# Turning each key head once, and copying it twice into the rows that the scores read

## The chip, the cores and the metric

The kernel runs on one core of one Trainium2 chip. The metric is the time of one execution on the device in microseconds (us). Five engines work side by side and meet at semaphores: PE multiplies matrices, DVE and ACT work on vectors, POOL does a few small steps, and SP's queue issues most DMA transfers. PE writes only to PSUM, which has eight banks; ACT and DVE move the results from there to SBUF. SBUF and PSUM have 128 partitions, called rows here where a matmul contracts over them.

## The reference

The program is a two-layer transformer trunk of width 1024, applied to two sequences, one of 256 and one of 512 positions. Layer A is a windowed attention with 16 query heads and 4 key heads of size 64; layer B is a differential attention with 8 heads, each with two queries and two keys of size 64. A gated feed-forward network follows each. What the change touches is how the scores are formed:

```
q = apply_rope(q, cos, sin) * (HEAD_DIM ** -0.5)
k = apply_rope(k, cos, sin)
...
sc = einsum('bqkgd,bskd->bkgqs', qi, kb)          # layer A, four queries share a key head
sc = einsum('bqhcd,bkhcd->bhcqk', qi, k)          # layer B, c = 0, 1: two queries, two keys
p  = softmax(sc);  a = p[:, :, 0] - lam * p[:, :, 1]
```

## The kernel before, in words

The 768 positions stand in six tiles of 128: tiles 0 and 1 are the first sequence, tiles 2 to 5 the second. Every product is made from two parts of each operand, a rounded part ("hi") and the rest ("lo"): hi x hi, lo x hi and hi x lo (`product_steps`, lines 313 to 317).

`mixer_a` and `mixer_b` both run over units i = (head group, tile), 24 units in A and 48 in B. A unit multiplies the tile's activations by the head's weights (24 matmuls of 384 columns into one bank, called `pqa` in A and `pqb` in B). Its `end` then does four things: ACT copies the values out of the bank (line 589, line 787), DVE rotates queries and keys (`rope`, lines 530 to 536, into `qk`), ACT writes the hi parts into a tile `sp` and DVE the lo parts (lines 594 to 599 in A, 794 to 799 in B). Two units later `turn` lets PE transpose the columns of `sp`, 128 by 128 at a time, into two banks, `tk` for keys and `tq` for queries (trace names `tka`, `tqa`, `tkb`, `tqb`), and ACT and DVE copy them to SBUF, where the scores read them.

How the parts lie matters. A score product contracts over 128 rows. In A a transposed query holds its hi part in rows 0 to 63 and its lo part in rows 64 to 127; so the key must stand in both halves: `kh` holds the key's hi part twice, and one product with it gives (hi + lo) x hi; `kl` holds the key's lo part twice. In B a head's two queries stand as (hi, lo) and (lo, hi), and the tile `kk` (trace name `kb`) holds three blocks: key 0's hi part twice, key 1's hi part twice, and key 0's and key 1's lo parts one above the other. In B `score` makes two products over 128 rows, one for each key (line 828), and two over 64 rows, one in the upper and one in the lower half (line 831). Before the change the doubling is done in `sp`: the parts are written there twice, and each doubled block is transposed.

A program written in this way passes through a scheduler when it is built: it puts each engine's instructions in an order that follows the source and the scheduler's own idea of when operands are ready. So a change of one helper can move instructions of other steps too. An engine then works through its own list strictly in that order, and an instruction that waits holds up what stands behind it.

In B the source places a unit's attention steps by the table `plan` (line 887). The four scores of the second sequence need the keys of all of tiles 2 to 5, so the first of these scores stands shortly after the turn of tile 5, in the unit of the next head's tile 1: this is called the head's boundary here.

Of the kernel before, what the change touches and what calls it, by code (L numbers as in the profile page):

```python
# [17 lines left out]
P = 128  # L18
D = 1024
KT = D // P  # L20
HD = 64
# [25 lines left out]
def trunk(  # L47
# [519 lines left out]
    def mixer_a(gp, g_next, first_steps, o):  # L567
        with ExitStack() as st:
# [4 lines left out]
            def unit(i):  # L573

                gi, t = divmod(i, NT)
                first, n = seq_of(t)
                if t == 0:
                    wk[gi] = column_blocks(take(4), HALF)
                elif t in (2, 4):
                    free(6 - t // 2)  # L580
                pm = bank(f"pqa_{i}")
                steps = product_steps(pm[:, :HALF], [(htile(t, k), wk[gi][k]) for k in range(KT)])
                if t == NT - 1:
                    steps = releasing(steps, 4, 2)

                def end():
                    if t == first:
                        vv[gi, first] = ap.tile([P, n, HD], F32, tag=f"v{first}", name=f"va{gi}_{first}", bufs=2)
                    nc.scalar.copy(out=vv[gi, first][:, t - first], in_=pm[:, 320:384])
                    qk = ap.tile([P, 5, HD], F32, tag="qk", name=f"qk{i}", bufs=2)  # L590
                    rope(ap, qk, pm[:, :320].rearrange("p (n d) -> p n d", d=HD), 5, t, f"a{i}")

                    sp = ap.tile([P, 6, 2, HD], F32R, tag="sp", name=f"sp{i}", bufs=2)
                    nc.scalar.copy(out=sp[:, 0:4, 0], in_=qk[:, 0:4])
                    nc.scalar.copy(out=sp[:, 4], in_=qk[:, 4:5].broadcast_to([P, 2, HD]))
                    nc.vector.tensor_tensor(
                        out=sp[:, 0:4, 1], in0=qk[:, 0:4], in1=sp.bitcast(F32)[:, 0:4, 0], op=ALU.subtract)
                    nc.vector.tensor_tensor(
                        out=sp[:, 5], in0=qk[:, 4:5].broadcast_to([P, 2, HD]), in1=sp.bitcast(F32)[:, 4], op=ALU.subtract)

                    def turn():
                        if t == first:
                            kh[gi, first] = ap.tile([P, n * P], F32R, tag=f"kh{first}", name=f"kha{gi}_{first}")
                            kl[gi, first] = ap.tile([P, n * P], F32R, tag=f"kl{first}", name=f"kla{gi}_{first}")
                        q[i] = ap.tile([P, 4, P], F32R, tag="q", name=f"qa{i}", bufs=4)
                        tq, tk = ps.tile([P, 512], F32R, tag="ps", name=f"tqa{i}"), ps.tile([P, 512], F32R, tag="ps", name=f"tka{i}")
                        at = slice((t - first) * P, (t - first + 1) * P)
                        for j in range(2):
                            nc.tensor.transpose(tk[:, j * P:(j + 1) * P], sp[:, 4 + j].rearrange("p a d -> p (a d)"), ident_r)
                        for j in range(4):  # L610
                            nc.tensor.transpose(tq[:, j * P:(j + 1) * P], sp[:, j].rearrange("p a d -> p (a d)"), ident_r)
                        nc.scalar.copy(out=kh[gi, first][:, at], in_=tk.bitcast(F32)[:, 0:P])
                        nc.scalar.copy(out=kl[gi, first][:, at], in_=tk.bitcast(F32)[:, P:2 * P])
                        nc.scalar.copy(out=q[i].rearrange("p h n -> p (h n)"), in_=tq.bitcast(F32))

                    pending[i] = turn

                return steps + [end]
# [146 lines left out]
    def mixer_b(gp, g_next, first_steps, o):  # L765
        with ExitStack() as st:
# [5 lines left out]
            def unit(i):  # L772

                h, t = divmod(i, NT)
                first, n = seq_of(t)
                if t == 0:
                    wk[h] = column_blocks(take(4), HALF)
                    free(4)
                pm = bank(f"pqb_{i}")
                steps = product_steps(pm[:, :HALF], [(htile(t, k), wk[h][k]) for k in range(KT)])  # L780
                if t == NT - 1:
                    steps = releasing(steps, 4)

                def end():
                    if t == first:
                        vv[h, first] = ap.tile([P, n, P], F32, tag=f"v{first}", name=f"vb{h}_{first}", bufs=2)
                    nc.scalar.copy(out=vv[h, first][:, t - first], in_=pm[:, 256:384])
                    qk = ap.tile([P, 4, HD], F32, tag="qk", name=f"bqk{i}", bufs=2)
                    rope(ap, qk, pm[:, :256].rearrange("p (n d) -> p n d", d=HD), 4, t, f"b{i}")

                    sp = ap.tile([P, 5, 2, HD], F32R, tag="sp", name=f"bsp{i}", bufs=2)
                    s4 = sp.rearrange("p a b d -> p (a b) d")
                    k2 = qk[:, 2:4].rearrange("p c (o d) -> p c o d", o=1).broadcast_to([P, 2, 2, HD])
                    nc.scalar.copy(out=s4[:, 0:4:3], in_=qk[:, 0:2])
                    nc.scalar.copy(out=sp[:, 2:4], in_=k2)
                    nc.vector.tensor_tensor(
                        out=s4[:, 1:3], in0=qk[:, 0:2], in1=s4.bitcast(F32)[:, 0:4:3], op=ALU.subtract)
                    nc.vector.tensor_tensor(
                        out=sp[:, 4], in0=qk[:, 2:4], in1=sp.bitcast(F32)[:, 2:4, 0], op=ALU.subtract)

                    def turn():
                        if t == first:
                            kk[h, first] = ap.tile([P, 3, n * P], F32R, tag=f"k{first}", name=f"kb{h}_{first}")
                        q[i] = ap.tile([P, 2, P], F32R, tag="q", name=f"qb{i}", bufs=5)
                        tq, tk = ps.tile([P, 512], F32R, tag="ps", name=f"tqb{i}"), ps.tile([P, 512], F32R, tag="ps", name=f"tkb{i}")
                        at = slice((t - first) * P, (t - first + 1) * P)
                        for j in range(3):
                            nc.tensor.transpose(tk[:, j * P:(j + 1) * P], sp[:, 2 + j].rearrange("p a d -> p (a d)"), ident_r)
                        for j in range(2):
                            nc.tensor.transpose(tq[:, j * P:(j + 1) * P], sp[:, j].rearrange("p a d -> p (a d)"), ident_r)  # L810
                        nc.scalar.copy(out=kk[h, first][:, :, at], in_=tk.bitcast(F32)[:, :3 * P].rearrange("p (k n) -> p k n", k=3))
                        nc.vector.tensor_copy(out=q[i].rearrange("p h n -> p (h n)"), in_=tq.bitcast(F32)[:, :256])

                    pending[i] = turn

                return steps + [end]
# [662 lines left out]
```

## Time and profile before

| | |
|---|---|
| median of 3 runs | 1687.2 us (1686.35 to 1689.65) |
| the profiled execution, its own time | 1688.34 us |
| its span, first to last instruction | 1686.6 us |
| mean granted PE clock | 0.997 |
| transposes of layer A's units (lines 609 and 611), seen from 25.7 to 224.7 us | 48 + 96 |
| transposes of layer B's units (lines 808 and 810), seen from 807.1 to 1113.7 us | 144 + 96 |
| score products of layer B (lines 828 and 831) | 96 + 96 |

The line numbers are those of the kernel before, and all times are counted from the first instruction. In the profile PEld is PE's loading of weights, which runs beside its matmuls; a matmul's duration reaches beyond the start of the next one, since matmuls are pipelined. So what one matmul costs PE is read from start to start.

### The profile page before, as it was taken

The page shows a single profiled execution, that of the slowest core. Times are in us where ns is not written, and L with a number is a line of the kernel's source. Part 1 is how long each engine was busy: PE and PEld are TensorE (multiplying, and loading weights), DVE is VectorE, ACT ScalarE, POOL GpSimd, SP SyncE. Part 2 cuts the span into 40 slices and gives each one's busy share as a digit, 9 for nine tenths or more (in the row PEclk, how much of TensorE's full clock was granted, in tenths as well). Part 3 has the DMA queues.
Part 4 walks back from the last instruction along what each step waited for, and adds up shares of the span by engine and source line. Part 5 has one row for each costly group of instructions (what it writes and reads, how often), then busy time and mean ns, then how long its engine had stood idle before and what let it go on. Part 6 is the DMA issues. An engine that isn't in the chain of part 4 may idle for free. (4 is left out here: it accounts for less than half of the span.)

```text
span 1686.6 us, 25513 instructions
## 1 busy us (share of the span) xinstructions
PE 1659.1 (98%) x9483; PEld 1514.3 (90%) x9483; DVE 1251.3 (74%) x2488; ACT 949.7 (56%) x2158; POOL 81.7 (5%) x104
## 2 busy tenths in 40 slices
PE   7999999999999999999999999999899999999998
PEld 7888878899999998888999999988799999998887
DVE  7888766896766666988777676874997666666886
ACT  6777775654444444556566666674744444444553
POOL 1000001000000000001000000331000000000001
PEclk9999999999999999999999999999999999999999
DMA  6111014534333347666211111113444343336765
GB/s 212 39 38 48 14 38 150 175 134 140 109 125 99 128 139 250 230 235 205 83 39 38 38 38 38 48 51 113 170 138 141 108 141 108 128 114 226 249 222 176
DMA packets 62107, 207.30 MB, mean 123 GB/s; under 512 B 6752, under 2 KB 8928, under 8 KB 61728
## 3 DMA queue, kind: packets, MB, share of 16 engines
q1 hardware_dynamic: 55152, 175.15, 30.8%
q0 software_dynamic: 6688, 30.28, 5.6%
q8 instruction: 74, 1.21, 0.3%
q14 instruction: 49, 0.40, 0.1%
q10 hardware_dynamic: 144, 0.26, 0.0%
HBM read 162.80 MB, written 42.86 MB: 122 GB/s over the span
## 5 line engine op out<-in xcount | busy, mean ns | idle before, releaser
L223 DVE TENSOR_TENSOR wlo<-wraw,whi 128x1024 fp32r<-128x1024 f32 (+2 forms) x180 | 204.9, 1144 | 173.9 <-ACT whi L222 172.7
L222 ACT CAST whi<-wraw 128x1024 fp32r<-128x1024 f32 (+2 forms) x180 | 176.5, 986 | 117.4 <-PE py L316 58.9
L315 PE MATMUL py<-hhi,whi 128*128 128x384 f32 x464 | 155.4, 335 | 0.8 <-ACT u L976 0.8
L317 PE MATMUL py<-hhi,wlo 128*128 128x384 f32 x464 | 155.0, 334 | 0.0
L316 PE MATMUL py<-hlo,whi 128*128 128x384 f32 x464 | 155.0, 334 | 0.0
L315 PE MATMUL pqb<-whi,hhi 128*128 128x384 f32 x384 | 136.5, 356 | 0.0
L316 PE MATMUL pqb<-wlo,hhi 128*128 128x384 f32 x384 | 128.9, 336 | 0.0
L317 PE MATMUL pqb<-whi,hlo 128*128 128x384 f32 x384 | 128.8, 335 | 0.0
L303 ACT CAST hhi<-araw 128x768 fp32r<-128x768 f32 (+1 forms) x74 | 57.6, 783 | 94.6 <-DMA araw<-act 94.2
L317 PE MATMUL pv<-whi,hlo 128*128 128x512 f32 (+1 forms) x240 | 92.2, 384 | 0.4 <-DVE hlo L304 0.4
L315 PE MATMUL pv<-whi,hhi 128*128 128x512 f32 (+1 forms) x240 | 92.4, 385 | 0.0
L316 PE MATMUL pv<-wlo,hhi 128*128 128x512 f32 (+1 forms) x240 | 92.1, 384 | 0.0
L304 DVE TENSOR_TENSOR hlo<-araw,hhi 128x768 fp32r<-128x768 f32 (+1 forms) x74 | 65.2, 889 | 32.3 <-ACT hhi L303 32.1
L315 PEld LDWEIGHTS py<-hhi,whi 128*128 128x128 f32 x464 | 87.1, 188 | 1.7 <-ACT u L976 1.4
L316 PEld LDWEIGHTS py<-hlo,whi 128*128 128x128 f32 x464 | 87.1, 188 | 0.0
L317 PEld LDWEIGHTS py<-hhi,wlo 128*128 128x128 f32 x464 | 87.1, 188 | 0.0
L315 PE MATMUL po<-whi,hhi 128*128 128x512 f32 x192 | 77.9, 406 | 0.2 <-ACT hhi L303 0.2
L317 PE MATMUL po<-whi,hlo 128*128 128x512 f32 x192 | 75.4, 393 | 0.2 <-DVE hlo L304 0.2
L316 PE MATMUL po<-wlo,hhi 128*128 128x512 f32 x192 | 75.3, 392 | 0.0
L315 PEld LDWEIGHTS pqb<-whi,hhi 128*128 128x128 f32 x384 | 72.3, 188 | 2.0 <-issue 1.7
L315 PE MATMUL pqa<-whi,hhi 128*128 128x384 f32 x192 | 73.9, 385 | 0.0
L315 PE MATMUL px<-hhi,whi 128*128 128x384 f32 x208 | 70.8, 342 | 2.7 <-ACT hhi L303 2.7
(303 smaller groups left out, 4829.6 us busy)
## 6 DMA issues: line engine op xcount, KB each, us to landing
act<-st POOLq DMA_DIRECT2D x22, 1344.0 KB, 6.6
wraw<-in_wgu SPq DMA_DIRECT2D x56, 512.0 KB, 4.6
araw<-act SPq DMA_DIRECT2D x70, 384.0 KB, 4.0
y_wraw<-in_wgu SPq DMA_DIRECT2D x40, 512.0 KB, 3.6
wraw<-in_wd SPq DMA_DIRECT2D x40, 512.0 KB, 3.9
wraw<-in_wb SPq DMA_DIRECT2D x32, 384.0 KB, 3.2
xd<-x SPq DMA_DIRECT2D x18, 512.0 KB, 3.0
x<-xd SPq DMA_DIRECT2D x18, 512.0 KB, 4.1
```

Source lines behind the costliest of these rows:

```text
L222: state["raw_hi"] = nc.scalar.copy(out=hi, in_=src)
L223: state["raw_lo"] = nc.vector.tensor_tensor(out=lo, in0=src, in1=hi.bitcast(F32), op=ALU.subtract)
L303: state["hi"] = nc.scalar.copy(out=hi, in_=src)
L304: state["lo"] = nc.vector.tensor_tensor(out=lo, in0=src, in1=hi.bitcast(F32), op=ALU.subtract)
L315: nc.tensor.matmul(out, ah, bh, start=start and i == 0, stop=False, skip_group_check=more)
L316: nc.tensor.matmul(out, ah, bl, start=False, stop=False, skip_group_check=more)
L317: nc.tensor.matmul(out, al, bh, start=False, stop=stop and i == last, skip_group_check=more)
```

## The change

In A the tile `sp` holds five blocks instead of six: each of the four queries, and the key, as (hi, lo). One ACT cast writes all hi parts and one DVE subtraction all lo parts. The key's one block is transposed once; its upper half is then copied twice, to the upper and the lower rows of `kh`, and its lower half twice to `kl`: three copies on ACT, one on DVE. Before there were two copies of all 128 rows on ACT.

In B `sp` holds four blocks instead of five: (hi, lo) and (lo, hi) of the queries, the hi parts of both keys side by side, and their lo parts. Two blocks instead of three are transposed into `tk`. The lo block is copied as it is (ACT); the hi block's halves are copied twice each, once by ACT and once by DVE. Before there was one copy of three blocks on ACT.

```
-                    sp = ap.tile([P, 6, 2, HD], F32R, tag="sp", name=f"sp{i}", bufs=2)
-                    nc.scalar.copy(out=sp[:, 0:4, 0], in_=qk[:, 0:4])
-                    nc.scalar.copy(out=sp[:, 4], in_=qk[:, 4:5].broadcast_to([P, 2, HD]))
-                    nc.vector.tensor_tensor(
-                        out=sp[:, 0:4, 1], in0=qk[:, 0:4], in1=sp.bitcast(F32)[:, 0:4, 0], op=ALU.subtract)
-                    nc.vector.tensor_tensor(
-                        out=sp[:, 5], in0=qk[:, 4:5].broadcast_to([P, 2, HD]), in1=sp.bitcast(F32)[:, 4], op=ALU.subtract)
+                    sp = ap.tile([P, 5, 2, HD], F32R, tag="sp", name=f"sp{i}", bufs=2)
+                    nc.scalar.copy(out=sp[:, :, 0], in_=qk)
+                    nc.vector.tensor_tensor(out=sp[:, :, 1], in0=qk, in1=sp.bitcast(F32)[:, :, 0], op=ALU.subtract)
...
-                        for j in range(2):
-                            nc.tensor.transpose(tk[:, j * P:(j + 1) * P], sp[:, 4 + j].rearrange("p a d -> p (a d)"), ident_r)
+                        nc.tensor.transpose(tk[:, :P], sp[:, 4].rearrange("p a d -> p (a d)"), ident_r)
...
-                        nc.scalar.copy(out=kh[gi, first][:, at], in_=tk.bitcast(F32)[:, 0:P])
-                        nc.scalar.copy(out=kl[gi, first][:, at], in_=tk.bitcast(F32)[:, P:2 * P])
+                        tkf = tk.bitcast(F32)
+                        nc.scalar.copy(out=kh[gi, first][:HD, at], in_=tkf[:HD, :P])
+                        nc.scalar.copy(out=kh[gi, first][HD:, at], in_=tkf[:HD, :P])
+                        nc.scalar.copy(out=kl[gi, first][:HD, at], in_=tkf[HD:, :P])
+                        nc.vector.tensor_copy(out=kl[gi, first][HD:, at], in_=tkf[HD:, :P])
...
-                    sp = ap.tile([P, 5, 2, HD], F32R, tag="sp", name=f"bsp{i}", bufs=2)
+                    sp = ap.tile([P, 4, 2, HD], F32R, tag="sp", name=f"bsp{i}", bufs=2)
-                    k2 = qk[:, 2:4].rearrange("p c (o d) -> p c o d", o=1).broadcast_to([P, 2, 2, HD])
-                    nc.scalar.copy(out=sp[:, 2:4], in_=k2)
+                    nc.scalar.copy(out=sp[:, 2], in_=qk[:, 2:4])
-                        out=sp[:, 4], in0=qk[:, 2:4], in1=sp.bitcast(F32)[:, 2:4, 0], op=ALU.subtract)
+                        out=sp[:, 3], in0=qk[:, 2:4], in1=sp.bitcast(F32)[:, 2], op=ALU.subtract)
...
-                        for j in range(3):
+                        for j in range(2):
                             nc.tensor.transpose(tk[:, j * P:(j + 1) * P], sp[:, 2 + j].rearrange("p a d -> p (a d)"), ident_r)
...
-                        nc.scalar.copy(out=kk[h, first][:, :, at], in_=tk.bitcast(F32)[:, :3 * P].rearrange("p (k n) -> p k n", k=3))
+                        tkf, k3 = tk.bitcast(F32), kk[h, first]
+                        nc.scalar.copy(out=k3[:, 2, at], in_=tkf[:, P:2 * P])
+                        nc.scalar.copy(out=k3[:HD, 0, at], in_=tkf[:HD, :P])
+                        nc.vector.tensor_copy(out=k3[HD:, 0, at], in_=tkf[:HD, :P])
+                        nc.scalar.copy(out=k3[:HD, 1, at], in_=tkf[HD:, :P])
+                        nc.vector.tensor_copy(out=k3[HD:, 1, at], in_=tkf[HD:, :P])
```

Because the scheduler decides, the change also moves instructions. On PE, at the first boundary of B (end of head 0's second sequence, inside the next head's unit `pqb`), the built order before is this, where F is used below for line 828 (128 rows) and L for line 831 (64 rows):

```order
L808 MATMUL tkb_9005<-ident_r,bsp_8920 128x128 x3
L810 MATMUL tqb_9004<-ident_r,bsp_8920 128x128 x2
L315 MATMUL pqb_8990<-whi_8882,hhi_111 128x384
L316 MATMUL pqb_8990<-wlo_8883,hhi_111 128x384
L317 MATMUL pqb_8990<-whi_8882,hlo_113 128x384
L315 MATMUL pqb_8990<-whi_8882,hhi_111 128x384
L316 MATMUL pqb_8990<-wlo_8883,hhi_111 128x384
L317 MATMUL pqb_8990<-whi_8882,hlo_113 128x384
L828 MATMUL bsc_0_9021<-kb_2_8775,qb_8776 128x512
L828 MATMUL bsc_1_9022<-kb_2_8775,qb_8776 128x512
L831 MATMUL bsc_0_9021<-kb_2_8775,qb_8776 128x512
L831 MATMUL bsc_1_9022<-kb_2_8775,qb_8776 128x512
```

The four products of a score stand F F L L, and the two L follow each other. After the change the same place reads:

```order
L806 MATMUL tkb_8996<-ident_r,bsp_8908 128x128 x2
L808 MATMUL tqb_8995<-ident_r,bsp_8908 128x128 x2
L315 MATMUL pqb_8981<-whi_8870,hhi_111 128x384
L316 MATMUL pqb_8981<-wlo_8871,hhi_111 128x384
L317 MATMUL pqb_8981<-whi_8870,hlo_113 128x384
L315 MATMUL pqb_8981<-whi_8870,hhi_111 128x384
L316 MATMUL pqb_8981<-wlo_8871,hhi_111 128x384
L317 MATMUL pqb_8981<-whi_8870,hlo_113 128x384
L832 MATMUL bsc_0_9015<-kb_2_8757,qb_8758 128x512
L835 MATMUL bsc_0_9015<-kb_2_8757,qb_8758 128x512
L315 MATMUL pqb_8981<-whi_8882,hhi_111 128x384
L832 MATMUL bsc_1_9016<-kb_2_8757,qb_8758 128x512
```

One transpose is gone, and the score is pulled apart: F and L of the first key, one product of the unit, then F and L of the second key. Over all of B, 48 scores stood F F L L before (32 with 512 columns, 16 with 256). After the change 40 still do; six with 512 columns stand F L F L, one with 512 columns stands F L, a product of the unit, F L (the place shown), and one with 256 columns stands F L F L. On PE the matmuls of all other kinds are the same in number, and nearly the same in order.

On ACT, at the same place, the order with what each instruction waits for is before:

```order
L794 CAST bsp_8985<-bqk_8978 128x2x64 [waits DVE_49]
L795 CAST bsp_8985<-bqk_8978 128x256
L811 CAST kb_2_8775<-tkb_9005 128x3x128 [waits PE_49]
L875 ACTIVATE ob_8518<-pob_9040,rden_8874 128x128 [waits PE_49]
L877 ACTIVATE sq_9044,ssh_8531<-ob_8518 128x128 [waits Activation_49]
```

and after the change:

```order
L811 CAST kb_2_8757<-tkb_8996 128x128 [waits PE_49]
L812 CAST kb_2_8757<-tkb_8996 64x128
L792 CAST bsp_8976<-bqk_8969 128x2x64 [waits DVE_49]
L793 CAST bsp_8976<-bqk_8969 128x128
L814 CAST kb_2_8757<-tkb_8996 64x128 [waits DVE_49]
L879 ACTIVATE ob_8494<-pob_9034,rden_8862 128x128 [waits PE_49]
```

The casts of the next unit's `bsp` now stand between the copies, and ACT's last copy waits for DVE. On DVE the place reads, after the change:

```order
L816 CAST qb_8994<-tqb_8995 128x256 [waits PE_49]
L813 CAST kb_2_8757<-tkb_8996 64x128 [waits Activation_49]
L794 TENSOR_TENSOR bsp_8976<-bqk_8969,bsp_8976 128x128 [waits Activation_49]
L796 TENSOR_TENSOR bsp_8976<-bqk_8969,bsp_8976 128x128 [waits Activation_49]
L815 CAST kb_2_8757<-tkb_8996 64x128 [waits Activation_49]
```

Both new copies on DVE wait for ACT; before, DVE had no copy of `tkb` at all. So the copies of one bank go from ACT (two) to DVE, to ACT and to DVE, one after the other.

## The prediction

> **What bounds the kernel now.** I read the page's engine shares first, then the stages the change touches, then what PE waits for there.
>
> ```profile
> span 1686.6 us, 25513 instructions
> PE 1659.1 (98%) x9483; PEld 1514.3 (90%) x9483; DVE 1251.3 (74%) x2488; ACT 949.7 (56%) x2158; POOL 81.7 (5%) x104
> ```
>
> A share over the whole span says little about two stages, so here is busy time by stretch: layer A's units (14.9 to 217) and layer B's (792.5 to 1105), the columns being the stretch, its length, and the busy time of PE, weight load, DVE, ACT, POOL, then clock, DMA share and GB/s.
>
> ```profile
> 14.90:217.00 202.10, 201.70 (x1410) 174.63 (x1409) 166.69 (x596) 152.10 (x529) 2.29 (x4) 1.00 0.18 57
> 792.50:1105.00 312.50, 312.44 (x2012) 288.11 (x2010) 228.55 (x679) 197.09 (x595) 22.93 (x16) 1.00 0.17 52
> ```
>
> PE is never idle in B (312.44 of 312.50 us) and hardly in A; DVE is busy for 73% of B and ACT for 63%. A view of what PE waited for, over 14 to 238 us, names three waits of 0.2 us, and over 1105 to 1126 us, where B ends, one:
>
> ```profile
> PE pqa L317 <- DVE hlo L304: 0.2, 1, 0.2
> ...
> PE tp_o L407 <- POOL ob L884: 0.6, 1, 0.6
> ```
>
> So both stages run at the rate at which PE starts one matmul after another. A matmul taken away is worth the distance between two starts; work added on ACT and DVE costs nothing until PE comes to wait for it.
>
> **Term 1: 72 transposes fewer.** A loses one in each of 24 units, B one in each of 48. The price is read from start to start, not from the 0.22 us that one lasts. Single transposes of a turn in B, from narrow windows of the timeline (start, duration):
>
> ```profile
> 829.30 0.22 PE L808 MATMUL tkb<-ident_r,bsp 128*128 128x128 f32 x1
> 829.36 0.32 PE L808 MATMUL tkb<-ident_r,bsp 128*128 128x128 f32 x2
> 829.51 0.25 PE L810 MATMUL tqb<-ident_r,bsp 128*128 128x128 f32 x1
> 829.69 0.41 PE L315 MATMUL pqb<-whi,hhi 128*128 128x384 f32 x1
> ```
>
> and of a turn in A:
>
> ```profile
> 106.57 0.36 PE L609 MATMUL tka<-ident_r,sp 128*128 128x128 f32 x2
> 106.77 0.50 PE L611 MATMUL tqa<-ident_r,sp 128*128 128x128 f32 x4
> 107.11 0.41 PE L316 MATMUL pqa<-wlo,hhi 128*128 128x384 f32 x1
> ```
>
> In B the second transpose starts 0.06 us after the first; the third and the ones for the queries are 0.09 apart (829.51 to 829.69 for two). In A the four for the queries take 0.34, or 0.085 each. The first starts are cheap because they follow a long matmul; a shorter row keeps them and loses one of the later ones. I take 0.085: 72 x 0.085 = 6.1 us saved. Ends: 0.06 each gives 4.3, 0.09 gives 6.5.
>
> **Term 2: eight scores of B in another order.** The built order pulls apart seven scores of 512 columns and one of 256 (F is the product over 128 rows, L the one over 64): F F L L becomes F L F L. What F F L L costs now:
>
> ```profile
> 830.80 0.39 PE L828 MATMUL bsc<-kb,qb 128*128 128x512 f32 x1
> 831.03 0.40 PE L828 MATMUL bsc<-kb,qb 128*128 128x512 f32 x1
> 831.36 0.49 PE L831 MATMUL bsc<-kb,qb 64*128 64x512 f32 x2
> 831.78 0.71 PE L871 MATMUL pob<-vb,aT 128*128 128x128 f32 x4
> ```
>
> F to F is 0.23 us, F to L 0.33, and both L together last 0.49: they run at the same time, on different rows. From them to the next matmul over 128 rows it is 0.42; in all 0.98. In the new order no two L are neighbours, so nothing runs beside either, and the two changes of row count become four: 0.33 + 0.42 + 0.33 + 0.42 = 1.50, so 0.52 more. Seven of these are 3.6 us. The form with 256 columns:
>
> ```profile
> 856.19 0.46 PE L828 MATMUL bsc<-kb,qb 128*128 128x256 f32 x2
> 856.58 0.39 PE L831 MATMUL bsc<-kb,qb 64*128 64x256 f32 x2
> 856.90 0.66 PE L859 MATMUL tpa<-ident,be 128*128 128x128 f32 x4
> ```
>
> takes 0.39 for both F and 0.32 for both L. With half of 0.39 for an F and the 0.32 for each L it becomes 1.03, 0.3 more. Term 2 is 3.9 us lost. The trace has no L followed by an F of the same score, so both ends: below, a change of rows costs nothing and each of the four takes F's 0.23, 0.92 in all, no loss; above, each waits for the end of the one before, 0.39 + 0.49 + 0.40 + 0.49 = 1.77, so 0.79 more, 5.5 us for seven and 6.0 with the small one. I take 3.9, since F to L and L to another matmul are both measured, and only the sequence is new.
>
> **Term 3: ACT and DVE.** Rows of the groups in B (792.5 to 1126), then in A (14 to 238); columns: count, then busy us, mean ns, idle before and its releaser.
>
> ```profile
> L811 ACT CAST kb<-tkb 128x384 fp32r<-128x384 f32 x48 | 22.9, 476 | 24.9 <-PE tkb L808 24.3
> L795 ACT CAST bsp<-bqk 128x256 fp32r<-128x256 f32 x48 | 19.3, 402 | 0.0
> L794 ACT CAST bsp<-bqk 128x128 fp32r<-128x128 f32 x48 | 14.3, 298 | 18.3 <-DVE bqk L536 17.0
> ...
> L223 DVE TENSOR_TENSOR wlo<-wraw,whi 128x768 fp32r<-128x768 f32 (+1 forms) x35 | 35.3, 1023 | 9.2 <-ACT whi L222 9.1
> L530 DVE TENSOR_TENSOR r_b<-pqb,cos_sb 128x256 f32<-128x256 f32 x48 | 20.2, 421 | 10.9 <-ACT vb L787 10.9
> L798 DVE TENSOR_TENSOR bsp<-bqk,bsp 128x128 fp32r<-128x128 f32 x48 | 13.8, 287 | 0.2
> ```
>
> ```profile
> L594 ACT CAST sp<-qk 128x256 fp32r<-128x256 f32 x24 | 9.8, 408 | 10.9 <-DVE qk L536 10.9
> L595 ACT CAST sp<-qk 128x128 fp32r<-128x128 f32 x24 | 7.2, 299 | 0.0
> L613 ACT CAST kla<-tka 128x128 fp32r<-128x128 f32 x24 | 6.7, 278 | 0.0
> L612 ACT CAST kha<-tka 128x128 fp32r<-128x128 f32 x24 | 6.5, 270 | 0.1
> ...
> L596 DVE TENSOR_TENSOR sp<-qk,sp 128x256 fp32r<-128x256 f32 x24 | 10.1, 420 | 1.1 <-ACT sp L594 0.9
> L598 DVE TENSOR_TENSOR sp<-qk,sp 128x128 fp32r<-128x128 f32 x24 | 6.8, 285 | 0.0
> ```
>
> A copy of 64 rows has as many columns as one of 128, so I price it by its columns: 0.27 on ACT (lines 612 and 613), 0.29 on DVE (line 798). B, each unit: ACT loses 0.476 + 0.402 and gains 3 x 0.27 + 0.298, 0.23 more, 11 us over 48 units; DVE gains two copies, 0.58, 28 us. ACT then has 208 and DVE 256 busy of 312 us. A, each unit: ACT loses 0.408 + 0.299 + 0.278 + 0.270 = 1.26 and gains a cast of 320 columns (about 0.46, from lines 594 and 595) and three copies, 1.27; DVE loses 0.705 and gains 0.49 and 0.29, 0.08 more, 2 us. All that lies under PE, with DVE at 82% of B.
>
> A wait can come where PE needs a copy soon. That is a boundary: the score starts at 830.80, 1.5 us after its turn. There the copies are now a chain, since ACT and DVE take turns on one bank; the trace has this already, where rotation (L530) sits idle 10.9 us for ACT's copy out of the same bank. The engines at the boundary before:
>
> ```profile
> 829.00 0.30 ACT L794 CAST bsp<-bqk 128x128 fp32r<-128x128 f32 x1 [1.04 <-DVE bqk L536]
> 829.21 0.40 ACT L795 CAST bsp<-bqk 128x256 fp32r<-128x256 f32 x1
> 829.71 0.48 ACT L811 CAST kb<-tkb 128x384 fp32r<-128x384 f32 x1
> ...
> 829.89 0.42 DVE L812 CAST qb<-tqb 128x256 fp32r<-128x256 f32 x1 [0.26 <-PE tqb L810]
> ```
>
> One copy ends at 830.19, 0.6 us before the score. In the new order, on this clock: two transposes end near 829.6, ACT's two copies (starts 0.21 apart, as 829.00 and 829.21) are done at 830.1; DVE first copies the queries (830.2) and then makes its first copy, done at 830.45; ACT, past two casts, makes its third by 830.8; DVE, past two subtractions, its second by 831.1. PE wants the first key at 830.7 and the second, after F and L (0.33 + 0.42), at 831.45. Both are there, with 0.25 and 0.35 to spare. I put term 3 at 0.3 us for small slips; its low end is 0, because PE shows no idle time in B that could shrink; its high end is the third rival. No DMA moves.
>
> **Sum.** -6.1 + 3.9 + 0.3 = -1.9 us. The profiled execution took 1688.34 us, 1.7 around its span; it becomes 1686.4. It lies 1.1 above the median of the runs, 1687.2, which becomes 1685.3.
>
> **Rivals.** *The order costs nothing.* PE loads weights for different rows ahead, and F L F L takes what F F L L took: -6.1 + 0.3, 1681.4 us. For it: F to L is only 0.33 where F lasts 0.39, so the two overlap. Against: L to the next matmul is 0.42, nearly twice F to F, and the pair's overlap is lost by any reading.
>
> *Each change of row count empties PE.* Term 2 at its upper end: -6.1 + 6.0 + 0.3, 1687.4 us. For it: the 0.42. Against: the 0.33, which is less than a whole F. The Trainium skill, "TensorEngine Tiling (Array Packing)", Key Properties, says that changing the tiling mode drains the engine while tiles of one mode run in parallel. The trace agrees on the second half (both L in 0.49), and half on the first, and that is why this rival has more than a small chance.
>
> *The chain of copies comes late (slower).* At a boundary, DVE has a subtraction of a weight tile (line 223, 1.02 us) in hand when ACT's copies are done. The first copy on DVE is then up to 1.02 late, ACT stands behind it at its third copy, and the score, with 0.3 to spare, stops PE. The whole 1.02 at seven boundaries is 7.1: -1.9 + 7.1, 1692.4 us. It decides the sign once a boundary loses 0.3 us, and makes the kernel slower by more than 0.2% from about 0.75. For it: DVE at 82%, two new hand-overs in each unit. Against: at the boundary shown no such subtraction stands near.
>
> **How the numbers follow.** Forecast 0.50, order free 0.17, emptied PE 0.17, late chain 0.16. The time is the forecast's, 1685.3. The range, 1681.0 to 1690.0, takes in the first two rivals and the mild half of the third. 0.2%, 3.4 us, is about what a measurement of this kernel can tell from no change. Faster than 1683.8: the first rival and a fifth of the forecast's cases (term 1 at 6.5, term 2 nearer 2), 0.27. Slower than 1690.6: most of the third, 0.13. Within: 0.60.
>
> **What would show it.** Right: 24 transposes for keys in A and 96 in B, their turns 0.085 shorter; at the seven boundaries F L F L taking 1.5 us; PE still busy for all but some tenths of B, now 0.2 us shorter, and A 2 us shorter. Wrong: an F L F L near 1.0 or 1.8 us, PE waiting for L814's or L815's copies, or for weights or `be` that DVE brings late.

## The result, and the profile after

The changed kernel takes 1696.7 us (median of 4 runs, 1695.5 to 1700.0), the kernel before beside it 1687.0: a ratio of 1.0053, with an interval of 1.0036 to 1.0069. A second comparison gave 1695.7 against 1689.2 us, 1.0042 (1.0029 to 1.0054). So the change costs 6.5 to 9.7 us. The forecast was 1685.3, in a range that ended at 1690.0. Single runs of one kernel lie some us apart (before: 1685 to 1695 over all comparisons), so the experiments below are read from their ratios and, within a trace, from the start of one and the same matmul in two traces.

The changed kernel's page has these shares; the second fence is its busy time by stretch, with the columns and the two stretches of the prediction:

```profile
span 1693.5 us, 25598 instructions
...
PE 1658.6 (98%) x9411; PEld 1508.4 (89%) x9411; DVE 1288.9 (76%) x2584; ACT 961.2 (57%) x2254; POOL 78.4 (5%) x104
```

```profile
14.90:217.00 202.10, 200.58 (x1391) 173.36 (x1389) 172.79 (x596) 158.17 (x529) 2.20 (x4) 1.00 0.19 60
792.50:1105.00 312.50, 310.28 (x1941) 281.71 (x1939) 254.83 (x764) 199.23 (x674) 19.93 (x13) 1.00 0.17 50
```

PE has 72 matmuls fewer (9483 to 9411). DVE is as busy in B as forecast (255 us, forecast 256), and ACT is less busy (199, forecast 208), in part because the forecast added up whole durations, while two copies in a row overlap (in the tail below they start 0.15 us apart and last 0.25). But PE, which was idle for 0.06 us of B's stretch, is now idle for 2.2. What it waited for from 790 to 1130 us (total, times, longest):

```profile
PE bsc L832 <- DVE kb L815: 1.6, 2, 1.4
PE bsc L832 <- DVE kb L813: 1.4, 2, 1.0
PE tkb L806 <- ACT bsp L793: 0.9, 1, 0.9
PE tqb L808 <- DVE bsp L794: 0.3, 1, 0.3
```

In the changed kernel 806 and 808 are the transposes, 811, 812 and 814 ACT's copies of the keys, 813 and 815 DVE's, 832 and 835 the score products (F and L below). Scores wait for DVE's copies four times, 3.0 us in all, at three places: at 1071.6 us, which is the boundary of head 6 inside the last head, at 1090.7 in the last head, and at 1118.3 in the tail, the steps behind the last unit. The other two rows are no key copies: there the last units' transposes wait for the parts of `bsp`, and the run with the last head in the old way, below, still has 1.0 us of that.

To see where the time goes, the table gives the start of the same matmul in each trace less its start in the trace before, in us, set to zero at B's first unit, so that it holds B and what follows alone. Each row is one trace, and one execution can lie some us off its kernel's median. Where an experiment moves scores, a matmul of the last head has more or less work ahead of it than in before, so these columns say little there; the last columns do not have this fault. The columns are places of the program, headed by their time in the trace before; the rows are the changed kernel, twice, and experiments that follow.

| kernel | unit 43, 1068 | unit 46, 1090 | behind the last unit, 1112 | first score of the tail done, 1115.5 | 1128.6 | 1165.6 | 1678.6 |
|---|---|---|---|---|---|---|---|
| changed | +1.3 | +4.5 | +3.6 | +6.9 | +8.1 | +9.8 | +9.2 |
| changed, again | +1.1 | +5.2 | +4.6 | +7.7 | +7.3 | +8.8 | +9.7 |
| last head in the old way | +1.2 | +2.2 | +2.2 | +3.1 | +3.1 | +3.0 | +2.3 |
| one hand-over | -0.5 | +4.8 | +4.4 | +8.5 | +9.9 | +9.9 | +11.0 |
| all copies on ACT | -2.7 | -1.5 | -2.8 | -0.5 | -0.8 | -1.0 | -1.6 |
| last seven units' copies on ACT | +1.1 | +2.4 | +1.0 | +3.3 | +2.9 | +4.0 | +5.2 |
| all scores later | -2.6 | -2.9 | +1.0 | +0.4 | +2.2 | +3.3 | +4.1 |
| before, scores later | 0.0 | -2.0 | +2.4 | +1.4 | +3.2 | +3.1 | +3.9 |
| last seven units old, boundaries later | -2.6 | -2.6 | -2.4 | -2.0 | -2.0 | -2.1 | -1.5 |

Up to unit 43, the second of the last head, the changed kernel has lost 1.3 us in B. In the five units after it and the tail behind them, 100 us of 1687, it loses 7 to 9 more.

### The profile page after: what moved, and what is told of

The parts are those of the page before. It is cut to its first block, busy times and chain, and to the rows that moved or that the text cites. A ratio compares the mean times of both kernels' runs of the same rounds, so it can differ in the third digit from the quotient of the medians.

```text
span 1693.5 us, 25598 instructions
## 1 busy us (share of the span) xinstructions
PE 1658.6 (98%) x9411; PEld 1508.4 (89%) x9411; DVE 1288.9 (76%) x2584; ACT 961.2 (57%) x2254; POOL 78.4 (5%) x104
## 3 DMA queue, kind: packets, MB, share of 16 engines
q8 instruction: 74, 1.21, 0.3%
## 5 line engine op out<-in xcount | busy, mean ns | idle before, releaser
L316 PEld LDWEIGHTS pqb<-wlo,hhi 128*128 128x128 f32 x384 | 72.4, 188 | 0.7 <-DVE wlo L223 0.6
```

The lines of the kernel that those rows point to most:

```text
L316: nc.tensor.matmul(out, ah, bl, start=False, stop=False, skip_group_check=more)
```

## What happens in the last head and the tail

The source places the last head's scores by a table of its own (`last_plan`): the first of them, of 256 columns, stands in the unit of tile 3, just behind the turn that makes its second key block, where other heads leave it until the next unit. The scores of the second sequence stand in a hand-written list behind the last unit, right after its turn. The timeline of the changed kernel at the first of these places (start, duration; in brackets idle time and what ended it):

```profile
1088.64 0.39 PE L832 MATMUL bsc<-kb,qb 128*128 128x256 f32 x1
1088.95 0.38 PE L835 MATMUL bsc<-kb,qb 64*128 64x256 f32 x1
1090.70 0.36 PE L832 MATMUL bsc<-kb,qb 128*128 128x256 f32 x1 [1.36 <-DVE kb L815]
...
1088.80 0.69 ACT L841 ACTIVATE be<-bsc,bmx 128x512 f32<-128x512 f32 x1
...
1089.60 0.26 ACT L814 CAST kb<-tkb 64x128 fp32r<-64x128 f32 x1
...
1088.30 0.28 DVE L813 CAST kb<-tkb 64x128 fp32r<-64x128 f32 x1
...
1089.61 0.17 DVE L846 RECIPROCAL rden<-bden 128x2 f32<-128x2 f32 x1 [0.51 <-ACT be L841]
...
1090.26 0.29 DVE L815 CAST kb<-tkb 64x128 fp32r<-64x128 f32 x1
```

ACT's third copy could go at 1088.6, when DVE's first is done; it stands behind a step of a norm and an exponential until 1089.60. DVE's second copy then stands behind a reciprocal that waits for that exponential, and behind two steps more. PE has made F and L of the first key by 1089.3 and waits 1.36 us for the second. And in the tail:

```profile
1118.27 0.46 PE L832 MATMUL bsc<-kb,qb 128*128 128x512 f32 x1 [1.04 <-DVE kb L813]
...
1117.25 0.26 ACT L812 CAST kb<-tkb 64x128 fp32r<-64x128 f32 x1
1117.40 0.68 ACT L414 ACTIVATE hhi<-tp_o,subl 128x512 fp32r<-128x512 f32 x1
1118.16 0.26 ACT L814 CAST kb<-tkb 64x128 fp32r<-64x128 f32 x1
...
1117.13 0.68 DVE L560 TENSOR_TENSOR ob<-po,gpost 128x512 f32<-128x512 f32 x1
1117.84 0.28 DVE L813 CAST kb<-tkb 64x128 fp32r<-64x128 f32 x1
1118.16 0.75 DVE L415 SCALAR_TENSOR_TENSOR hlo<-tp_o,subl,hhi 128x512 fp32r<-128x512 f32 x1
1118.94 0.29 DVE L815 CAST kb<-tkb 64x128 fp32r<-64x128 f32 x1
```

Between the links of the chain of copies stand steps of the output projection: 560 ahead of DVE's first copy, 414 ahead of ACT's third, 415 ahead of DVE's second. Those on DVE set the time: 560 ends at 1117.81 and 415 at 1118.91, and DVE's copies start 0.03 us behind each, while 414 is done at 1118.08, before DVE's first copy is (1118.12). From ACT's first copy (1117.10) to the end of DVE's last (1119.23) it takes 2.13 us; before, one copy of 0.48 did it. The Trainium skill, "PSUM — Partial Sum Buffer", Engine vs sequencer instructions, says that the queues of ACT, DVE and POOL are strictly first in, first out; the trace agrees, since 813 and 815 go only after the steps ahead of them.

Behind that stall the granted clock falls. Busy time by stretch, the clock being the third number from the end:

```profile
1116.00:1118.00 2.00, 0.94 (x8) 0.65 (x7) 1.91 (x7) 1.78 (x6) 0.00 (x0) 1.00 0.42 100
1118.00:1120.00 2.00, 1.51 (x4) 0.74 (x4) 1.86 (x4) 0.35 (x2) 0.00 (x0) 1.00 0.40 162
1120.00:1122.00 2.00, 2.00 (x6) 1.48 (x6) 0.88 (x3) 0.90 (x3) 0.00 (x0) 0.68 0.00 0
1122.00:1124.00 2.00, 2.00 (x6) 1.52 (x6) 1.14 (x3) 0.55 (x2) 0.00 (x0) 0.50 0.00 0
1124.00:1126.00 2.00, 2.00 (x10) 1.19 (x9) 0.96 (x2) 0.00 (x0) 0.00 (x0) 0.97 0.00 0
```

For 4 us PE makes six matmuls in 2 us where ten went. Counted as in the table, its matmuls are 6.88 us behind before where the fall starts and 8.43 where it ends, 1.55 more. Last, between 1160 and 1170 us, PE waits for the two parts of a weight tile of the projection, which ACT and DVE split there, as it did not before:

```profile
PE po L316 <- DVE wlo L223: 0.8, 1, 0.8
PE po L315 <- ACT whi L222: 0.5, 1, 0.5
```

That is most of the table's step from 8.1 to 9.8; why the tile came late was not tried.

## The experiments

**A alone.** `mixer_a` of the changed kernel, `mixer_b` of the kernel before.

> Only layer A is changed; layer B is as before. The theory (the loss is in layer B, in its last head and the tail behind it): 24 transposes fewer by 0.085 us make A's stage about 2 us shorter, and the time is about 1685 us, 2 below before. The rival (the copies by halves cost PE waits in both layers): A gains nothing or loses, 1687 to 1690 us.

Measured: 1686.5 against 1688.9 us, 0.9984 (0.9973 to 0.9994), 2.4 us below. The gain in A is there, as sized.

**B alone.** The other way round.

> Only layer B is changed; layer A is as before. The theory: all of the loss is here and A's gain of 2 us is missing, so the time is about 9 to 12 us above before, 1696 to 1699 us. The rival (both layers lose alike): about half of the loss, some 5 us above before, 1692 us.

Measured: 1695.6 against 1688.9, 1.0040 (1.0027 to 1.0053): 6.7 us above, less than the 9 to 12 expected, but the loss is in B.

**The last head in the old way.** In B, for the last 6 of the 48 units:

```
+ once = h < 7
+ nb = 2 if once else 3      # blocks that are transposed
  ... split, transposes and copies as in the change if once, else as before
```

> The changed kernel, but the last head of B (6 of its 48 units) is split, transposed and copied in the old way. The theory (the loss sits in the last head and the tail, where the copies stand behind exponentials and splits, PE waits and the granted clock then falls): some 7 us of the loss go, 1688 to 1690 us, and the clock stays at 1.00 where it fell to 0.5. The rival (the loss is spread over all heads: the order F L F L at each boundary, the heavier DVE): seven eighths of the loss stay, about 1695 us.

Measured: 1687.2 against 1688.9, 0.9992 (0.9984 to 1.0001). That is 0.0050 of the time, 8.4 us, below the changed kernel's 1.0042. Six transposes come back (0.5 us) and two F L F L go (1.1), so 7.8 us are the late copies and what follows from them; by the intervals of the two ratios it could be 5 to 10. The table gives 6.3 and 6.8 in the same way, from the 6.9 and 7.4 us between the last columns. In this trace the clock stays at 1.00 from 1115 to 1125 us.

**The order alone.** The kernel before, with F L F L written for all 48 scores:

```
  for c in range(2):
-     nc.tensor.matmul(ss[c], q[i][:, c], kk[h, first][:, c], start=True, stop=False)
-
- for c, rows in enumerate((slice(0, HD), slice(HD, P))):
+     rows = (slice(0, HD), slice(HD, P))[c]
+     nc.tensor.matmul(ss[c], q[i][:, c], kk[h, first][:, c], start=True, stop=False)
      nc.tensor.matmul(ss[c], q[i][rows, c], kk[h, first][rows, 2], start=False, stop=True)
```

> The kernel before with nothing changed but the order of its score products in B: F L F L is written for all 48 scores, 32 of 512 columns and 16 of 256, so that the cost of the order stands alone with no copies in it. By the prediction's term (0.52 and 0.3 us each): 32 x 0.52 + 16 x 0.3 = 21 us above before. If the order is free: no change. If each change of row count empties PE (0.79 and 0.5): 33 us above.

Measured: 1715.1 against 1688.9, 1.0156 (1.0143 to 1.0170), 26 us above: between the prediction's term and the emptied PE. One score of 512 columns and one of 256 in this trace, with the matmul that follows:

```profile
838.50 0.40 PE L828 MATMUL bsc<-kb,qb 128*128 128x512 f32 x1
838.83 0.50 PE L829 MATMUL bsc<-kb,qb 64*128 64x512 f32 x1
839.26 0.49 PE L828 MATMUL bsc<-kb,qb 128*128 128x512 f32 x1
839.68 0.50 PE L829 MATMUL bsc<-kb,qb 64*128 64x512 f32 x1
840.11 0.66 PE L857 MATMUL tpa<-ident,be 128*128 128x128 f32 x4
...
857.34 0.34 PE L828 MATMUL bsc<-kb,qb 128*128 128x256 f32 x1
...
858.55 0.66 PE L857 MATMUL tpa<-ident,be 128*128 128x128 f32 x4
```

0.33 + 0.43 + 0.42 + 0.43 = 1.61 us, 0.63 more than F F L L; the small form 1.21, 0.50 more. From unit to unit the shifts against before say 0.64 and 0.50. For 32 and 16 scores that is 28.5 us, at the upper end of the measured interval (24 to 29).

**The last head's scores later.** In `last_plan` the score of tile 0 goes from place 9 of unit 3 to place 2 of unit 4, and in the tail's list three products are taken ahead of the first score:

```
- last_plan.update({1: ((2 - NT, 8),), 3: ((5 - NT, 4), (0, 9)), 4: ((1, 3),), 5: ()})
+ last_plan.update({1: ((2 - NT, 8),), 3: ((5 - NT, 4),), 4: ((0, 2), (1, 5)), 5: ()})
- run += do(score, s0) + out[1][:3] + do(score, s1) + out[1][3:5] + ...
+ run += out[1][:3] + do(score, s0) + out[1][3:4] + do(score, s1) + out[1][4:5] + ...
```

> The changed kernel with the scores of B's last head one to three products later: the first one, of 256 columns, 3 places later, and the first two behind the last unit 3 and 1 places later. Copies, transposes and five of the seven orders F L F L stay. The theory (in the last head and the tail PE comes for the copies before they are done, because the plan puts a score right behind the turn that feeds it, and only there): the waits and the fall of the granted clock go; what is left is 96 transposes' worth of rows, 72 x 0.085 = 6.1 us gained, five F L F L at 0.64 = 3.2 and the pulled-apart score some 0.7 lost, so 1.5 to 2.5 us below before. The rival (the copies cost ACT and DVE time, and the last head is short of that, wherever the scores stand): 4 us or more of the loss stay, 3 to 6 above before.

Measured: 1690.8 against 1689.2, 1.0014 (1.0004 to 1.0024). Better than the changed kernel beside it (1.0042), but not what the theory said: in the trace, which is of the slowest of its nine runs (1695.2), PE now waits 2.1 us for `aT`, the exponentials turned, which come late because their scores do. The same wait stands in the trace of before with the scores later, below (2.4 us).

**All scores later.** The same, and the boundary score of every head goes from place 7 to 8 (`1: ((2 - NT, 8),)`), which brings back F F L L everywhere.

> As the run with the last head's scores later, and the boundary score of each other head one place later as well, by which all 48 scores of the built order are F F L L again. The change itself (24 and 48 transposes fewer, copies by halves on ACT and DVE) is whole. The theory: nothing is left but the transposes that are gone, so 5 to 7 us below before (ratio 0.996 to 0.997), faster than both kernels. The rival (later scores make the exponentials, their transposes and the tail late in turn): no better than 2 us below before.

Measured: 1689.0 against 1689.2, 1.0001 (0.9992 to 1.0011). The table's trace tells why: from unit 8 to unit 43 its 35 turns gain 2.86 us, 0.082 each, just what was forecast; the last head and the tail give back more than that. The first eight units are not in this figure: they lose 0.2 us where their turns should gain 0.7, and the trace names one wait of 0.2 there, for an exponential that DVE has in hand (`be`). The rest of that was not looked into.

**Before, with the scores later.** The same two tables in the kernel before.

> The kernel before, with its scores moved as in the run in which all scores stand later; transposes and copies are as before. That run kept 5.5 us of gain up to the last head and lost 6.7 behind it. If the later scores themselves cost that (the exponentials and what follows them come late in turn): 4 to 6 us above before. If the copies by halves cost it, wherever the scores stand: within 1 us of before.

Measured: 1693.2 against 1688.8, 1.0021 (1.0009 to 1.0033), 3.5 us above by the ratio and 4.4 by the medians, about what was expected (4 to 6) if the later scores themselves cost it. So nearly 4 of the 6.7 us that the last run lost there (from -2.6 to +4.1 in the table; here 3.9) are the price of its own cure.

**One hand-over.** The order of the five copies: ACT's three first, then DVE's two.

```
- ACT (lo), ACT (key 0), DVE (key 0), ACT (key 1), DVE (key 1)
+ ACT (key 0), ACT (key 1), ACT (lo), DVE (key 0), DVE (key 1)
```

> The changed kernel with the five copies of a key tile in B in another order: ACT makes its three first, then DVE its two, so the bank goes over once and not three times. The built order has one F L F L of 512 columns and one of 256, and one score pulled apart, where the change has six, one and one. If the hand-overs make the copies late: the waits in the last head and the tail go, and 5 x 0.64 = 3.2 us for the order, so 1 to 2 us below before. If they are late because they stand behind exponentials and splits in ACT's and DVE's queues: only the 3.2 us go, 2 to 5 us above before.

Measured: 1694.1 against 1689.2, 1.0036 (1.0023 to 1.0048): nothing of the waits went. PE waits 6.7 us in B and the tail, against 4.4 in the changed kernel, and the time is only 1.5 us lower, although five scores that stand F F L L again are worth 3.2. In the tail DVE reads in this trace:

```profile
1117.88 0.68 DVE L560 TENSOR_TENSOR ob<-po,gpost 128x512 f32<-128x512 f32 x1
1118.59 0.28 DVE L814 CAST kb<-tkb 64x128 fp32r<-64x128 f32 x1
1118.91 0.29 DVE L815 CAST kb<-tkb 64x128 fp32r<-64x128 f32 x1
```

ACT's last copy was done at 1118.2; DVE's two, together now, still stand behind 560. The number of hand-overs is not what makes them late.

**All copies on ACT.** `nc.vector.tensor_copy` becomes `nc.scalar.copy` for the keys, in A and B.

> The changed kernel with all copies of the keys on ACT and none on DVE, in both layers. The built order then has one F L F L of 512 columns and one of 256, the other 46 scores are F F L L. If the hand-overs between ACT and DVE, or DVE's load, make the copies late: the waits of the last head and the tail go and it is 3 to 5 us below before. If the copies are late because five follow one another behind other work, on whatever engine: PE waits for ACT in the last head and the tail as long as it did for DVE, and it is 1 to 4 us above before, the order's 3.2 us better than the change.

Measured: 1686.1 against 1688.8, 0.9980 (0.9972 to 0.9989): 2.7 us below, close to the first reading. Beside the changed kernel's 6.5 above that is 9.2 us, of which six scores that stand F F L L again are some 3.8. ACT in the tail, at the place shown above:

```profile
1112.00 0.25 ACT L811 CAST kb<-tkb 128x128 fp32r<-128x128 f32 x1
1112.15 0.26 ACT L812 CAST kb<-tkb 64x128 fp32r<-64x128 f32 x1
1112.42 0.26 ACT L813 CAST kb<-tkb 64x128 fp32r<-64x128 f32 x1
1112.70 0.26 ACT L814 CAST kb<-tkb 64x128 fp32r<-64x128 f32 x1
1112.97 0.26 ACT L815 CAST kb<-tkb 64x128 fp32r<-64x128 f32 x1
```

The same five copies, all on one engine, take 1.23 us and not 2.13, because nothing stands between them. PE waits 0.8 us there, and the clock does not fall.

**The last seven units' copies on ACT.** As the last run, but for units 41 to 47 alone and in B alone; the order of the scores is that of the change.

> The changed kernel with the key copies of B's last seven units all on ACT; the other 41 units copy on ACT and DVE as in the change, and the order of the scores is that of the change (six F L F L, one pulled apart, one small F L F L). If DVE's part in the copies is what loses the time in the last head and the tail: the loss behind unit 43 falls from 7 to 9 us to the 2 us that the run with all copies on ACT kept, and the time is 4 to 6 us below the changed kernel's, 0 to 3 us above before. If that run was better for its order of scores alone: no more than 1 us below the changed kernel's.

Measured: 1690.9 against 1689.0, 1.0006 (0.9995 to 1.0016). 0.0036 of the time, 6 us by the ratios and 4.7 by the medians, below the changed kernel. So DVE's part in seven units of 48 is 4 to 6 us of the loss, apart from any order. It is not all: in the table this trace still loses 4.1 us behind unit 43, where 2 were expected and the changed kernel loses 7.9 and 8.6. Of PE's waits in B the largest left is

```profile
PE bsc L833 <- ACT kb L814: 1.5, 2, 0.8
```

**POOL's multiplication on DVE.** Why is DVE late at unit 43 too, where no projection stands in its queue? Rows of DVE, PE and POOL of the changed kernel:

```profile
1069.28 1.32 DVE L794 TENSOR_TENSOR bsp<-bqk,bsp 128x128 fp32r<-128x128 f32 x1 [0.37 <-ACT bsp L792]
...
1071.17 0.28 DVE L813 CAST kb<-tkb 64x128 fp32r<-64x128 f32 x1
...
1076.72 1.78 DVE L794 TENSOR_TENSOR bsp<-bqk,bsp 128x128 fp32r<-128x128 f32 x1
...
1071.61 0.47 PE L832 MATMUL bsc<-kb,qb 128*128 128x512 f32 x1 [0.38 <-DVE kb L813]
...
1068.66 1.80 POOL L888 TENSOR_TENSOR ob<-ob,rstd_sub 128x896 f32<-128x896 f32 x1
...
1076.65 1.70 POOL L888 TENSOR_TENSOR ob<-ob,rstd_sub 128x896 f32<-128x896 f32 x1
```

A subtraction that lasts 0.28 us elsewhere lasts until POOL's multiplication ends (1070.46 and 1070.60, 1078.35 and 1078.50). The Trainium skill, "SBUF — State Buffer", SBUF: two separate sides, says that a DVE instruction with two SBUF inputs and a POOL instruction that reads SBUF exclude each other for the whole instruction; the trace agrees. DVE's first key copy stands behind the first of these, and PE waits for it; from unit 43 to unit 44 the changed kernel falls 0.96 us further behind before. Behind the second PE does not wait. The experiment puts line 888 on DVE:

```
- nc.gpsimd.tensor_tensor(out=ov, in0=ov, in1=rb, op=ALU.mult)
+ nc.vector.tensor_tensor(out=ov, in0=ov, in1=rb, op=ALU.mult)
```

> The changed kernel, with the multiplication of B's outputs by their norm (line 888, in the last two heads, 128 x 896) on DVE in place of POOL. In the changed kernel's trace a DVE subtraction that starts while POOL multiplies lasts 1.3 to 1.8 us and not 0.28, and DVE's copies of the keys stand behind it. If that hold is what makes the copies late in the last head: no DVE instruction of 0.28 us is stretched any more, the 3.3 us that are lost from the last head's first unit to its last fall to 1 or 2, and the time is 1 to 2.5 us below the changed kernel's, 4 to 7 us above before. If the copies are late because of what stands ahead of them in any case: the multiplications (about 1 us each) stand in DVE's queue too, and it is as slow as the changed kernel or slower, 7 us or more above before. The tail behind the last unit, where POOL does not multiply, keeps its 4 to 5 us by both.

Its control is the same edit in the kernel before:

> The kernel before with the same move of the multiplications from POOL to DVE, so that the run above can be read without the move's own worth. In before no key copy is on DVE, and PE shows one wait of 0.6 us behind POOL's multiplication: 0 to 1 us below before if the hold costs PE nothing there.

Measured: 1.0078 (1.0066 to 1.0091) in the changed kernel, 13.6 us above before; 1.0011 (1.0001 to 1.0021) in the kernel before. The subtractions are back at 0.29 us, and it is much worse:

```profile
1064.84 0.28 DVE L813 CAST kb<-tkb 64x128 fp32r<-64x128 f32 x1
1066.84 1.09 DVE L888 TENSOR_TENSOR ob<-ob,rstd_sub 128x896 f32<-128x896 f32 x1 [1.72 <-POOL rstd_sub L360]
1067.96 0.29 DVE L815 CAST kb<-tkb 64x128 fp32r<-64x128 f32 x1
```

The multiplication waits 1.72 us for POOL's power and holds up the second key copy, which stood next. So the same edit costs 1.8 us where no key copy is on DVE and some 4 to 7 (13.6 less the 9.7 or 6.5 of the changed kernel) where two are; 0.6 of that is one more score that stands F L F L. How much the hold by POOL costs in the changed kernel by itself stays open beyond the 0.96 us at unit 43, since this edit put a longer wait in its place.

**Two versions with the old way where there is no slack.** In the first, units 41 to 47 are split, transposed and copied as before (`once = i < 41`) and the boundary scores of the other heads stand one place later (`1: ((2 - NT, 8),)`). In the second, the last tile of each head and all of the last head are in the old way (`once = h < 7 and t < 5`), and no score moves.

> The changed kernel, with the last seven units of B (the last tile of head 6 and all of head 7) in the old way, and the boundary score of the other heads one place later, so that all 48 scores are F F L L. 24 + 41 transposes fewer. The theory (nothing but the order at the boundaries and the late copies of the last head and the tail eats the gain): 65 x 0.085 = 5.5 us, so 4.5 to 5.5 us below before, ratio 0.997, faster than both kernels. The rival (the steady heads lose elsewhere too, or the tail is late with the old copies as well): less than 2 us below before.

> The changed kernel, with the last tile of each head and all of the last head in the old way; no score is moved, and all 48 are F F L L. 24 + 35 transposes fewer. The theory: 59 x 0.085 = 5.0 us below before, ratio 0.997. If the fall of the gain lies in the copies of every unit and not in those just before a score: less than 2 us below.

Measured: 1683.5 against 1688.8, 0.9969 (0.9959 to 0.9979), and 1684.8 against 1688.8, 0.9970 (0.9959 to 0.9981). Both beat the kernel before, by 4 to 5 us, and with the 6.5 us of the second comparison the changed one by 11 to 12; 65 and 59 transposes at 0.085 are 5.5 and 5.0.

## Why the prediction was wrong

*Term 1, the transposes, was right.* A alone gained 2.4 us where 2.0 was forecast; in B a turn gains 0.082 from unit 8 on where no score is out of order, and the two last versions gain what 0.085 for each transpose says.

*Term 2, the order, was right in its mechanism and too small.* An F L F L costs 0.64 us and not 0.52, a small one 0.50 and not 0.3. The term that was mis-sized is the second F to L: it was set at 0.33, like the one after F, and measured 0.42, behind an F that follows an L and lasts 0.49 instead of 0.40. With seven and one it is 5.0 us for 3.9. The prediction also put all seven at boundaries. In the trace six stand there (828.7 to 1030.3 us); the seventh is the first score of the tail (1118.3), and the small one is in the last head (1088.6). Those are two of the three places where PE then waited. The rival that each change of row count empties PE (0.79) is refuted as it was priced, and so is the free order: each change of rows takes 0.33 to 0.43 from start to start, less than the 0.40 to 0.50 that the matmul ahead of it lasts by the profile.

*Term 3, the waits, failed, and it alone turned the sign.* It was put at 0.3 us and is 6 to 8: 7.8 by the run with the last head in the old way, 6.3 and 6.8 by the table. In the changed kernel's first trace PE's waits for the copies are 3.0 us, the lower clock costs 1.55 and the late weights 1.3; the rest was not taken apart. The step that failed is "A wait can come where PE needs a copy soon. That is a boundary". The working for a boundary held, as the changed kernel's timeline at the second one shows:

```profile
869.06 0.47 PE L832 MATMUL bsc<-kb,qb 128*128 128x512 f32 x1
...
869.87 0.50 PE L832 MATMUL bsc<-kb,qb 128*128 128x512 f32 x1
...
868.62 0.28 DVE L813 CAST kb<-tkb 64x128 fp32r<-64x128 f32 x1
...
869.24 0.29 DVE L815 CAST kb<-tkb 64x128 fp32r<-64x128 f32 x1 [0.33 <-ACT kb L814]
```

The second copy is done at 869.53, 0.34 before PE wants it (0.35 was forecast). At the first six boundaries of this trace no score waits; at the seventh, in unit 43, one waits 0.38, and in the trace of B alone one waits 0.8 at the first, so the slack was thin. But the boundary was taken to be the only tight place. The last head has a plan of its own and the tail a list of its own, both in the source, and both put a score right behind its turn, while ACT and DVE also carry exponentials, norms and the projection's splits. No time was worked out for them; the waits of before were read there, one of 0.6 us, and so little was taken for slack.

*The third rival was nearest in time and right in kind.* It said that DVE has other work in hand when ACT's copies are done, that ACT then stands behind it at its third copy, and that PE stops: 1692.4 us. All of that happened, but at one of the seven boundaries alone, behind the subtraction that POOL held, and then once more in the last head and once in the tail, behind steps of attention and projection. Its price took the whole 1.02 us at each boundary, although it named 0.3 to spare; less that it is 5.0 us and 1690.3. Its 0.16 was too little, because its test ("no such subtraction stands near") was made at one boundary.

*Not foreseen* were what came behind the stalls in the first trace: 1.55 us of lower clock, and 1.3 us for weights further on.

By the measured terms the sum is -6.1 + 5.0 + 7.8 = +6.7 us, against 6.5 and 9.7 in the two comparisons. The 7.8 was itself taken from the comparison with 6.5, so what tests the first two terms is the run with the last head in the old way: 66 transposes and six scores make -5.6 + 3.8 = -1.8 us, and 1.7 us below before were measured. Of the experiments, the theory of the scores that stand too early was wrong in part: moving them moved the wait to what follows.

## What to carry to other kernels

A copy that is split between two in-order engines is as late as whatever stands between its links: five copies in a row on the engine that already made them took 1.23 us, the same five in turns 2.13, and before one 0.48. Work moved onto an engine with idle time must be followed to the place with the least slack, which is seldom the steady loop: look for the last iteration, its own plan and the tail, and work out there, row by row, when each link can start. Where a saving is good in 41 units and bad in 7, do it in the 41.

## What the runs showed of the hardware that was not expected

A stall can cost more than itself. In the changed kernel PE was busy for 0.94 and 1.51 of two stretches of 2 us, and the granted clock then stood at 0.68 and 0.50 for 4 us; its second execution had no such fall there, but one to 0.57 and 0.58 at 1092 to 1096 us, behind a wait of 1.37 us at 1091. The Trainium skill, "TensorE: Matmul & The Clock Gate", Part 1, ties the half clock to an idle window of about 3.4 us. Here the longest single wait of the four us ahead was 1.04 us, and PE worked on both sides of it, so here the clock fell behind a window that was only partly idle (PE busy for 2.45 of 4 us). Such a window does not bring it each time: with the last seven units' copies on ACT PE was also busy for 2.45 of the 4 us from 1110, and the clock stayed at 1.00 up to 1120. The place at which it falls changes from execution to execution.

POOL can hold DVE: a subtraction of 0.28 us lasted 1.32 and 1.78 us beside POOL's multiplications.

The order of two kinds of score products over 128 and 64 rows is worth 26 us over 48 scores of this kernel, with the same matmuls and the same bytes.
